# A gate projection by seven block products on one Trainium2 core: sums of h^T ahead of it, and weights split half a task sooner

## The chip, the cores and the metric

The kernel runs on one core of a Trainium2 chip. The metric is the time of one execution on the device, in microseconds (us), lower being better. The engines of the core are TensorE (PE in the profile; PEld is its weight load), VectorE (DVE), ScalarE (ACT), GpSimd (POOL) and SyncE (SP, which here only issues transfers). Each engine works through a queue of its own in a fixed order and waits on semaphores of the others.

## The reference

One layer for 1024 tokens of width 1024, in float32:

```
h = RMSNorm(x)
[q,k,v,z_a | u,z_s | g_a,g_s] = h @ W_in
y_a = BandAttn(q,k,v) * silu(z_a) @ W_attn_out
y_s = GLU(gelu(S5(u))) * silu(z_s) @ W_ssm_out
x = x + (sigmoid(g_a) * y_a + sigmoid(g_s) * y_s) @ W_out
out = RMSNorm(x)
```

The attention and y_a, y_s before their output products are 512 wide; g_a and g_s are 1024 wide. The part that the change rewrites is g_s = h @ W_gs, a product of 1024 by 1024 by 1024.

## The kernel before, in words

**Numbers.** Every large product is made of three matmuls on operands that were split into a rounded high part (hi = round(x), on ACT, line 100) and the rest (lo = x - hi, on DVE, line 103): hi*hi, lo*hi and hi*lo (lines 106 to 108). A weight or an activation is so split once before its use. The normed input is kept transposed as four tiles: hT_134 and hT_135 are the high parts for the halves 0 and 1 of the 1024 features (K), hT_136 and hT_137 the low parts. In a tile lie four K blocks r of 128 features, each with 1024 tokens.

**Tasks.** A projection task makes 128 output columns for all tokens: 8 K blocks x 2 token halves x 3 = 48 matmuls of 512 columns. Its weights come as one load of 512 KB (w_raw), are split into w_hi and w_lo (128x1024 each), and its two halves are evacuated from PSUM by ACT. After the band attention come three tasks for g_a (ga[5:8]), then eight for g_s (`gs_task`, line 1127), whose evacuation is a sigmoid on ACT and a store to DRAM (sgs_dr). Then come tasks with K = 512, of 2 x 4 x 3 = 24 matmuls and one 256 KB load each: 8 for y_a @ W_attn_out ("a tasks": `mm<-y_hi,o_hi` and so on; evacuated on DVE as mgd = mm * sigmoid(g_a)), 8 for the GLU, 8 for y_s @ W_ssm_out, which read the stored sigmoid(g_s) back. Last is the product with W_out, done by pairs of row tiles in seven block products of 12 matmuls (Strassen's scheme in Winograd's form); for it 28 tables `wb` of sums of W_out are made by POOL (sums t, wo_raw), ACT and DVE (splits) while the K = 512 tasks run.

**Stream.** `Stream.run` (line 160 on) keeps the weights of the next task ahead: it loads the raw weights at the start of a task and splits them in its first half (the second task of the 48-matmul kind, after 7 of 16 steps; a K = 512 task has two steps, and the split is put after the first). The splits have high priority.

**Order.** The tile framework sets the order of each engine's queue, from priorities and an estimate of its own; around the attention the kernel places the work by hand. What follows the attention (`issue_after(last_turn)`) is in the part that the framework orders.

Of the kernel before, what the change touches and what calls it, by code (L numbers as in the profile page):

```python
# [17 lines left out]
P = 128  # L18
L = 1024
# [25 lines left out]
def trunk_kernel(ctx: ExitStack, tc: tile.TileContext, x, x_t, ng, w_m, w_v, bias, a_re, a_im, log_dt,  # L45
# [38 lines left out]
    def tt(o, a, b, op, eng=None):  # L84
        (eng or vec).tensor_tensor(out=o, in0=a, in1=b, op=op)  # L85
# [13 lines left out]
    def split_hi(hi, src):  # L99
        act.activation(out=hi, in_=src, func=AF.Copy)  # L100

    def split_lo(lo, src, hi, eng=None):
        (eng or vec).tensor_tensor(out=lo, in0=src, in1=hi.bitcast(F32), op=SUB)  # L103
# [46 lines left out]
    class Stream:  # L150
# [952 lines left out]
    def o_task(src, y, evac, before=None, late=False):  # L1103
# [19 lines left out]
                evac(half, pss[half])  # L1123
                yield
        return (o_dma(src), o_split, run, 2)

    def gs_task(m):
        def evac(half, ps):
            sg = half_tile()
            act.activation(out=sg, in_=ps, func=AF.Sigmoid, bias=gb[:, KT + m:KT + m + 1])  # L1130
# [170 lines left out]
    MATES = {"P1": ("A11", "B11"), "P2": ("A12", "B21"), "P3": ("S4", "B22"), "P4": ("A22", "T4"),  # L1301
             "P5": ("S1", "T1"), "P6": ("S2", "T2"), "P7": ("S3", "T3")}
# [6 lines left out]
    def operand(src, pool_, tag):  # L1309
        t = pool_.tile([P, 2, 4, P], F32R, tag=tag, name="a")  # L1310
        split_hi(t[:, 0], src)
        split_lo(t[:, 1], src, t[:, 0])
        return t
# [12 lines left out]
    ORDER = [("P1", "a", (0,)), ("P2", "b", (0,)), ("P6", "a", (1,)), ("P5", "c", (3,)), ("P7", "a", (3,)),
             ("P3", "c", (1,)), ("P4", "a", (2,))]
# [7 lines left out]
    banks = [(ps_m, "mm")] * 3 + [(ps_2, "s")] * 2 + [(ps_t, "pt")] * 2  # L1341
    taken = [0]

    def bank():
        p_, tag = banks[taken[0] % 7]
        taken[0] += 1
        return p_.tile([P, HALF], F32, tag=tag, name="c")

    for n in range(KT // 2):
        first, last = n == 0, n == KT // 2 - 1  # L1350
        tok = [slice((2 * n + r) * P, (2 * n + r + 1) * P) for r in range(2)]
# [48 lines left out]
        for pn, bk, to in order:  # L1400
            an, bn = MATES[pn]
            if first and an in fin_op:
                a = fin_op[an]
            else:
                for d in DER.get(an, []):
                    derive(*d)
                a = operand(blk[an], vp, "v")
            new = bk not in pss
            if new:
                pss[bk] = bank()  # L1410
            ends = [b for b in to if parts[b] == 1]
            two = last and pn == "P4"
            cuts = [slice(0, HALF)] if not two else [slice(0, HALF // 2), slice(HALF // 2, HALF)]
            for cs in cuts:
                for k in range(4):
                    w = wb[bn, k]
                    o, h, l = pss[bk][:, cs], w[:, 0, cs], w[:, 1, cs]
                    pe.matmul(o, a[:, 0, k, :], h, start=new and k == 0, stop=False, skip_group_check=True)  # L1418
                    pe.matmul(o, a[:, 0, k, :], l, start=False, stop=False, skip_group_check=True)  # L1419
                    pe.matmul(o, a[:, 1, k, :], h, start=False, stop=k == 3, skip_group_check=True)  # L1420
# [84 lines left out]
```

## Time and profile before

| what | value |
|---|---|
| time, median of 3 runs | 810.49 us (809.4 to 811.29) |
| the profiled execution | 809.81 us, with a span of 808.0 us in its trace (1.8 us lie around the span) |
| PE | busy 787.5 us, 97% of the span, 3882 matmuls |
| DVE | busy 515.1 us, 64% |
| ACT | busy 371.4 us, 46% |
| POOL | busy 199.8 us, 25% |
| DMA | 94 GB/s on average |

A row of the timeline gives the start in us, the duration, the engine, the line, the operation, `out<-in` with buffer numbers left out, the size, and in brackets how long the engine had been idle before it and who released it. A matmul's end is modelled: matmuls overlap in the pipeline, so the distance between two starts, and not the duration, says what one costs. A row of the view by windows gives for each engine the busy time in the window and the number of instructions, then the granted PE clock, the share of DMA time and GB/s.

### The profile page before, as it was taken

The numbers are of one execution on the slowest core, as the hardware profiler recorded it, in microseconds if no ns is written. First come the engines' busy times: TensorE is split into PE (matmuls) and PEld (weight loads), VectorE is DVE, ScalarE is ACT, GpSimd is POOL, SyncE is SP. The second block draws the span as 40 slices with busy tenths as digits, with TensorE's granted clock in tenths as the row PEclk, the third lists the DMA queues.
The fourth block names the chain that finished last, engine by engine and source line by source line (L and its number), as shares of the span: only waits on it lengthen the run. The fifth ranks groups of instructions, "written<-read, shape, count | busy, mean of one in ns | idle before, by whom it ended". The sixth has DMA issues, their size and how long they took to land. (4 is left out here: it accounts for less than half of the span.)

```text
span 808.0 us, 11034 instructions
## 1 busy us (share of the span) xinstructions
PE 787.5 (97%) x3882; PEld 652.8 (81%) x3882; DVE 515.1 (64%) x1323; ACT 371.4 (46%) x669; POOL 199.8 (25%) x220
## 2 busy tenths in 40 slices
PE   8999999999999999999999999999999999999996
PEld 6778888888887888888888888888867887788884
DVE  6999997978647888788445430111178337865684
ACT  5653455646436566666444572222253224222542
POOL 4560022020202323333122100000023222844431
PEclk9999999999999999999999999999999999999999
DMA  8703433233331011111000261221144114432232
GB/s 310 263 28 105 116 86 119 90 84 129 102 117 43 27 43 43 44 43 43 27 27 27 79 209 66 104 105 66 52 131 157 52 44 140 132 103 104 104 131 79
DMA packets 37063, 76.22 MB, mean 94 GB/s; under 512 B 5072, under 2 KB 14288, under 8 KB 37008
## 3 DMA queue, kind: packets, MB, share of 16 engines
q1 hardware_dynamic: 32512, 69.74, 25.5%
q0 software_dynamic: 1152, 2.36, 1.4%
q10 hardware_dynamic: 3344, 3.42, 1.4%
q8 instruction: 30, 0.49, 0.3%
q14 instruction: 25, 0.20, 0.1%
HBM read 60.34 MB, written 15.17 MB: 93 GB/s over the span
## 5 line engine op out<-in xcount | busy, mean ns | idle before, releaser
L106 PE MATMUL mm<-hT,w_hi 128*128 128x512 f32 x576 | 233.3, 405 | 0.0
L108 PE MATMUL mm<-hT,w_lo 128*128 128x512 f32 x576 | 226.0, 392 | 0.7 <-DVE w_lo L103 0.7
L107 PE MATMUL mm<-hT,w_hi 128*128 128x512 f32 x576 | 225.4, 391 | 0.0
L108 PEld LDWEIGHTS mm<-hT,w_lo 128*128 128x128 f32 x576 | 108.1, 188 | 24.5 <-DVE w_lo L103 1.1
L107 PEld LDWEIGHTS mm<-hT,w_hi 128*128 128x128 f32 x576 | 108.6, 189 | 16.6 <-issue 0.4
L106 PEld LDWEIGHTS mm<-hT,w_hi 128*128 128x128 f32 x576 | 108.4, 188 | 16.2 <-issue 0.2
L103 DVE TENSOR_TENSOR w_lo<-w_raw,w_hi 128x1024 fp32r<-128x1024 f32 x36 | 44.3, 1230 | 83.7 <-ACT w_hi L100 83.5
L933 POOL TENSOR_SCALAR p<-p,sm 128x640 f32<-128x640 f32 (+2 forms) x64 | 42.8, 671 | 111.2 <-DVE sm L932 80.6
L100 ACT ACTIVATE w_hi<-w_raw 128x1024 fp32r<-128x1024 f32 x36 | 38.1, 1059 | 69.0 <-PE mm L107 58.4
L931 ACT ACTIVATE p<-p,mx 128x640 f32<-128x640 f32 (+2 forms) x64 | 44.5, 695 | 33.3 <-DVE mx L89 16.6
L103 DVE TENSOR_TENSOR tl<-pt,th 128x512 fp32r<-128x512 f32 (+2 forms) x72 | 43.1, 600 | 24.5 <-ACT th L100 23.9
L100 ACT ACTIVATE th<-pt 128x512 fp32r<-128x512 f32 (+2 forms) x72 | 37.7, 523 | 44.5 <-PE pt L951 43.9
L924 DVE CUSTOM_DVE_ANT_0 p<-s,bias 128x320 f32<-128x320 f32 (+2 forms) x96 | 44.2, 485 | 17.1 <-PE s L923 16.7
L106 PE MATMUL mm<-y_hi,o_hi 128*128 128x512 f32 x128 | 50.6, 398 | 3.1 <-DVE sg L85 1.5
L108 PE MATMUL mm<-y_hi,o_lo 128*128 128x512 f32 x128 | 50.5, 396 | 2.6 <-DVE o_lo L103 2.6
L107 PE MATMUL mm<-y_lo,o_hi 128*128 128x512 f32 x128 | 50.4, 394 | 0.0
L85 POOL TENSOR_TENSOR t<-wo_raw 128x512 f32<-128x512 f32 x8 | 11.3, 1409 | 148.7 <-PE mm L107 129.8
L1419 PE MATMUL c<-wb,a 128*128 128x512 f32 (+1 forms) x116 | 44.8, 387 | 0.0
L1418 PE MATMUL c<-wb,a 128*128 128x512 f32 (+1 forms) x116 | 44.1, 386 | 0.5 <-DVE x L85 0.5
L1420 PE MATMUL c<-wb,a 128*128 128x512 f32 (+1 forms) x116 | 44.2, 385 | 0.0
L951 PE MATMUL pt<-ident,p 128*128 128x128 f32 x240 | 38.1, 273 | 0.0
L970 PE MATMUL pv<-tl,vt 128*128 128x256 f32 x144 | 36.2, 281 | 1.0 <-DVE tl L103 1.0
(230 smaller groups left out, 1534.9 us busy)
## 6 DMA issues: line engine op xcount, KB each, us to landing
w_raw<-in_w_m_dram SPq DMA_DIRECT2D x36, 512.0 KB, 3.5
x<-in_x_dram SPq DMA_DIRECT2D x16, 512.0 KB, 7.6
sgs_dr<-sg SPq DMA_DIRECT2D x16, 256.0 KB, 2.0
wo_raw<-in_w_out_dram SPq DMA_DIRECT2D x8, 512.0 KB, 3.5
sg<-sgs_dr SPq DMA_DIRECT2D x16, 256.0 KB, 2.9
xt<-in_x_t_dram SPq DMA_DIRECT2D x6, 512.0 KB, 9.8
bias<-in_bias_dram SPq DMA_DIRECT2D x8, 320.0 KB, 2.9
wv_raw<-in_w_v_dram SPq DMA_DIRECT2D x8, 256.0 KB, 5.4
```

What stands on the lines that cost most here:

```text
L100: act.activation(out=hi, in_=src, func=AF.Copy)
L103: (eng or vec).tensor_tensor(out=lo, in0=src, in1=hi.bitcast(F32), op=SUB)
L106: pe.matmul(ps, lh, rh, start=first, stop=False)
L107: pe.matmul(ps, lh, rl, start=False, stop=False)
L108: pe.matmul(ps, ll, rh, start=False, stop=last)
L924: vec.tensor_tensor_reduce(out=pr[:, c * cw:(c + 1) * cw], in0=ps, in1=bt[:, 640 - w + c * cw:640 - w + (c + 1) * cw], scale=1.0, scalar=- ...
L931: act.activation(out=pr[:, :w], in_=pr[:, :w], func=AF.Exp, bias=mx[:, 0:1], accum_out=sm)
L933: pool.tensor_scalar(out=pr[:, :w], in0=pr[:, :w], scalar1=sm, scalar2=1.0, op0=MUL, op1=MUL)
L951: last_turn[0] = pe.transpose(tp[:, n:n + P], probs[h, q][:, k * P:(k + 1) * P], ident).ins
L1418: pe.matmul(o, a[:, 0, k, :], h, start=new and k == 0, stop=False, skip_group_check=True)
L1419: pe.matmul(o, a[:, 0, k, :], l, start=False, stop=False, skip_group_check=True)
L1420: pe.matmul(o, a[:, 1, k, :], h, start=False, stop=k == 3, skip_group_check=True)
```

## The change

1. The eight `gs_task` are gone. `gs_pairs` does g_s by pairs of column tiles: 4 pairs x 7 block products x 12 matmuls. The left operands are blocks of W_gs and sums of them (S1 to S4 of each pair, four POOL operations a pair), split as 512-wide operands `a`. The right operands are blocks of h^T (B11, B21, B22) and four sums of blocks: T1 = B12 - B11, T3 = B22 - B12, T2 = B22 - T1 and T4 = B21 - T2, each with hi and lo for four K blocks r.
2. `h_sums` makes T1, T2 and T3, a step every second step of the three g_a tasks; T1 and T2 lie in the room of the attention's v (pool vp, tag "v"), two of the T3 tiles in a small pool `gsp`. `h_last` makes T4 in the first four block products, over the second token half of hT_134 and hT_136, which no later product reads. The order of products is P1, P2, P6, P5, P7, P3, P4, where P5 is S1 by T1 and P6 is S2 by T2; the framework may put neighbours the other way round.
3. The evacuation of a block product is an ACT copy into an `sg` tile, a DVE addition (`sg<-c,sg`) or the final sigmoid on ACT.
4. `Stream`: where a K = 512 task follows a K = 512 task, the next weights are split ahead of the first half of the current task (`early`), not after it.
5. Around it: the splits of the attention's output (za, four of 128x1024 hi and lo) go from ahead of the g_a tasks to the 27th block product; the loads `yr` of the S5's output and the first a tasks' weights move with it; the steps at which its splits (`g_lo`) and the W_out tables are emitted shift by some places; the last `zs` tile is split in two halves.

```diff
+        def split(self, task):
+            with tc.high_priority():
+                self.w = task[1](self.raws.pop(id(task)))
...
+                early = ny == 2 and ahead and ahead[0][3] == 2
+                if early:
+                    self.split(ahead[0])
                 for i, _ in enumerate(run(w)):
-                    if i == max(ny // 2 - 1, 0) and ahead:
-                        with tc.high_priority():
-                            self.w = ahead[0][1](self.raws.pop(id(ahead[0])))
+                    if i == max(ny // 2 - 1, 0) and ahead and not early:
+                        self.split(ahead[0])
                     yield
...
-    def gs_task(m):
-        def evac(half, ps):
-            sg = half_tile()
-            act.activation(out=sg, in_=ps, func=AF.Sigmoid, bias=gb[:, KT + m:KT + m + 1])
-            nc.sync.dma_start(out=sgs_dr[m][:, cut(half)], in_=sg)
-        return proj_task(w_m[28 + m], evac)
...
+    def block_product(o, a, tab, cs, first):
+        for k in range(4):
+            h, l = tab(k)
+            pe.matmul(o, a[:, 0, k, :], h[:, cs], start=first and k == 0, stop=False, skip_group_check=True)
+            pe.matmul(o, a[:, 0, k, :], l[:, cs], start=False, stop=False, skip_group_check=True)
+            pe.matmul(o, a[:, 1, k, :], h[:, cs], start=False, stop=k == 3, skip_group_check=True)
...
+    def h_sum(tag, q, r, c, eng):
+
+        o = rest.tile([P, HALF], F32, tag=tag, name="hs")
+        tt(o, hT[0][q][:, r, cut(c)].bitcast(F32), hT[1][q][:, r, cut(c)].bitcast(F32), ADD, eng)
+        return o
+
+    def split_tab(tab, src):
+        split_hi(tab[0], src)
+        split_lo(tab[1], src, tab[0])
+
+    def h_sums():
+
+        for r in range(4):
+            b11 = h_sum("o_raw", 0, r, 0, vec)
+            b12 = h_sum("o_lo", 0, r, 1, vec)
+            b22 = h_sum("o_hi", 1, r, 1, pool)
+            yield
+            tt(b22, b22, b12, SUB, pool)
+            tt(b12, b12, b11, SUB)
+            yield
+            split_tab(h_tab("T3", r), b22)
+            tt(b11, b22, b11, ADD, pool)
+            yield
+            split_tab(h_tab("T1", r), b12)
+            yield
+            split_tab(h_tab("T2", r), b11)
+            yield
+
+    def h_last(r):
+
+        b21 = h_sum("o_raw", 1, r, 0, vec)
+        t2 = rest.tile([P, HALF], F32, tag="o_lo", name="hs")
+        th_, tl_ = h_tab("T2", r)
+        tt(t2, th_.bitcast(F32), tl_.bitcast(F32), ADD, pool)
+        tt(b21, b21, t2, SUB, vec)
+        split_tab(h_tab("T4", r), b21)
...
+        with tc.high_priority():
+            g_op[u] = operand(src.rearrange("p (k m) -> p k m", m=P), wp, tag)
+        if pn == "P2":
+
+            g_s1[n] = rest.tile([P, HALF], F32, tag="o_hi", name="s1")
+            a11, a12, a21, a22 = (g_block(b, n) for b in ("A11", "A12", "A21", "A22"))
+            tt(g_s1[n], a21, a22, ADD, pool)
+            tt(a21, a11, a21, SUB, pool)
+            tt(a11, g_s1[n], a11, SUB, pool)
+            tt(a12, a12, a11, SUB, pool)
+
+    def gs_pairs():
+
+        AHEAD = 2
+        for u in range(AHEAD):
+            g_operand(u)
+        yield
...
+            if u + AHEAD < steps:
+                g_operand(u + AHEAD)
+            if n == 0 and i < 4:
+                h_last(i)
+            new = (n, bk) not in pss
+            if new:
+                pss[n, bk] = bank()
+            ps = pss[n, bk]
+            block_product(ps, g_op.pop(u), lambda k: h_tab(MATES[pn][1], k), slice(0, HALF), new)
...
+    gen = stream.run(ga[NGA:])
+    sums = h_sums()
+    n_ga = len(ga[NGA:]) * 2 * KT
+    for n in range(n_ga):
+        with tc.issue_after(last_turn[0]) if n < 4 * KT else ExitStack():
             next(gen)
-    for b in range(2):
-        load_y(b)
+        if n % 2 == 1:
+            next(sums, None)
...
-    hs, ls = split_tiles(zs, vp, "v", "y")
+    hs, ls = split_tiles(zs, vp, "v", "y", (3,))
```

The order of three queues at the place where g_s begins. First DVE, from the last operation of the attention (`y<-pv,y`) on; `hs` are sums of blocks of h^T, `t_...` their splits into the tables. Before:

```order
985 L103 TENSOR_TENSOR w_lo<-w_raw,w_hi 128x1024
986 L85 TENSOR_TENSOR y<-pv,y 64x512
987 L103 TENSOR_TENSOR y_lo<-z,y_hi 128x1024
988 L103 TENSOR_TENSOR o_lo<-o_raw,o_hi 128x512 x2
989 L103 TENSOR_TENSOR w_lo<-w_raw,w_hi 128x1024 x9
```

In the changed kernel:

```order
981 L103 TENSOR_TENSOR w_lo<-w_raw,w_hi 128x1024
982 L85 TENSOR_TENSOR y<-pv,y 64x512
983 L85 TENSOR_TENSOR hs<-hT_134,hT_136 128x512 x4
984 L85 TENSOR_TENSOR hs<-hs 128x512
985 L103 TENSOR_TENSOR t_5183<-hs,t_5183 128x512
986 L85 TENSOR_TENSOR hs<-hs 128x512
```

And the end of what stands there ahead of the operands of the first pair's third and fourth product (`a<-g_raw,a` in row 1017 is S2 for P6, `a<-s_5430,a` in row 1018 is S1 for P5):

```order
1011 L85 TENSOR_TENSOR hs<-hT_135,hT_137 128x512
1012 L103 TENSOR_TENSOR hT_136<-hs,hT_134 128x512
1013 L85 TENSOR_TENSOR hs<-hs 128x512
1014 L85 TENSOR_TENSOR hs<-hT_135,hT_137 128x512
1015 L85 TENSOR_TENSOR hs<-hs 128x512
1016 L103 TENSOR_TENSOR hT_136<-hs,hT_134 128x512
1017 L103 TENSOR_TENSOR a<-g_raw,a 128x512
1018 L103 TENSOR_TENSOR a<-s_5430,a 128x512
```

Between the last `y` and the operand of P5 stood nothing; now stand 39 operations there (one of them the third g_a task's w_lo of 128x1024; rows with x4 or x2 are so many), and the operand is the 40th. The first operand of g_s (P1) is the 23rd.

POOL, from the last operation of the attention (`z<-z,y`) on. Before:

```order
107 L933 TENSOR_SCALAR p<-p,sm 128x640 x3
108 L85 TENSOR_TENSOR z<-z,y 64x512 x2
109 L85 TENSOR_TENSOR t<-wo_raw 128x512
110 L85 TENSOR_TENSOR wo_raw<-wo_raw 128x512
111 L85 TENSOR_TENSOR t<-wo_raw 128x512
```

Changed (`s_5430` is S1; the `g_raw<-s_5430,g_raw` of row 119 makes S2):

```order
108 L85 TENSOR_TENSOR z<-z,y 64x512 x2
109 L85 TENSOR_TENSOR hs<-hT_135,hT_137 128x512 x2
110 L85 TENSOR_TENSOR hs<-hs 128x512 x4
111 L85 TENSOR_TENSOR hs<-hT_135,hT_137 128x512 x2
112 L85 TENSOR_TENSOR hs<-hs 128x512 x3
113 L85 TENSOR_TENSOR hs<-t_5175 128x512
114 L85 TENSOR_TENSOR s_5430<-g_raw 128x512
115 L85 TENSOR_TENSOR hs<-hs 128x512
116 L85 TENSOR_TENSOR g_raw<-g_raw 128x512
117 L85 TENSOR_TENSOR hs<-t_5176 128x512
118 L85 TENSOR_TENSOR hs<-t_5177 128x512
119 L85 TENSOR_TENSOR g_raw<-s_5430,g_raw 128x512
```

Where POOL went from the attention straight to the tables of W_out, it now has 18 operations up to S2, all of 128x512 with both inputs in SBUF.

PE, 24 matmuls after the last g_a matmul. Before, in the first task of g_s:

```order
2217 L106 MATMUL mm<-hT_135,w_hi 128x512
2218 L107 MATMUL mm<-hT_137,w_hi 128x512
2219 L108 MATMUL mm<-hT_135,w_lo 128x512
2220 L106 MATMUL mm<-hT_134,w_hi 128x512
2221 L107 MATMUL mm<-hT_136,w_hi 128x512
```

Changed, where P2 ends and P5 begins, whose right operand is T1 (t_5179 and the three after it):

```order
2217 L1225 MATMUL c<-hT_135,a 128x512
2218 L1226 MATMUL c<-hT_137,a 128x512
2219 L1227 MATMUL c<-hT_135,a 128x512
2220 L1225 MATMUL c<-t_5179,a 128x512
2221 L1226 MATMUL c<-t_5179,a 128x512
```

P1 and P2 take h^T as it is; P5 stands third, with P6 after it, so that S1's operand is the first for which PE needs the end of the DVE rows above.

More of the change, by code (lines that the diff above doesn't have):

```diff
@@ L1070, in trunk_kernel, with split_tiles @@
     sgs_dr = [dr.tile([P, L], F32, name=f"sgs_dr{m}") for m in range(KT)]
+    gsp_cm = tc.tile_pool(name="gsp", reuse_waits="tile", bufs=2)
+    gsp = gsp_cm.__enter__()
+    half_pool = [gsp, 3]
     def half_tile():
-        return rest.tile([P, HALF], F32, tag="sg", name="sg", bufs=4)
+        return half_pool[0].tile([P, HALF], F32, tag="sg", name="sg", bufs=half_pool[1])
     def cut(half):
         return slice(half * HALF, (half + 1) * HALF)
-    def split_tiles(raws, pool_, tag, name):
+    def split_tiles(raws, pool_, tag, name, halves=()):
         hs, ls = [], []
-        for r in raws:
+        for n, r in enumerate(raws):
             hi = pool_.tile([P, L], F32R, tag=tag, name=name + "_hi")
             lo = pool_.tile([P, L], F32R, tag=tag, name=name + "_lo")
-            split_hi(hi, r)
-            split_lo(lo, r, hi)
+            for c in [cut(0), cut(1)] if n in halves else [slice(0, L)]:
+                split_hi(hi[:, c], r[:, c])
+                split_lo(lo[:, c], r[:, c], hi[:, c])
             hs.append(hi)
@@ new lines, in trunk_kernel, with bank, operand @@
+    taken = [0]
+    def bank():
+        p_, tag = banks[taken[0] % 7]
+        taken[0] += 1
+        return p_.tile([P, HALF], F32, tag=tag, name="c")
+    def operand(src, pool_, tag):
+        t = pool_.tile([P, 2, 4, P], F32R, tag=tag, name="a")
+        split_hi(t[:, 0], src)
+        split_lo(t[:, 1], src, t[:, 0])
+        return t
+    def block_product(o, a, tab, cs, first):
[4 more added lines that the diff above has]
+            pe.matmul(o, a[:, 1, k, :], h[:, cs], start=False, stop=k == 3, skip_group_check=True)
@@ new lines, in trunk_kernel, with h_tab @@
+    t2s = [vp.tile([P, 2, HALF], F32R, tag="v", name="t2") for _ in range(4)]
+    t1s = [vp.tile([P, 2, HALF], F32R, tag="v", name="t1") for _ in range(4)]
+    t3s = [qk_pools[1].tile([P, 2, HALF], F32R, tag="blk", name="t3") for _ in range(2)] + [
+        gsp.tile([P, 2, HALF], F32R, tag="t3", name="t3") for _ in range(2)]
+    def h_tab(name, r):
+        if name in ("B11", "B21", "B22", "T4"):
+            q, c = (0 if name in ("B11", "T4") else 1), cut(1 if name in ("B22", "T4") else 0)
+            return hT[0][q][:, r, c], hT[1][q][:, r, c]
+        t = {"T1": t1s, "T2": t2s, "T3": t3s}[name][r]
+        return t[:, 0, :], t[:, 1, :]
@@ new lines, in h_last, with g_load @@
+    def h_last(r):
[5 more added lines that the diff above has]
+        split_tab(h_tab("T4", r), b21)
+    g_raw = {}
+    def g_load(m):
+        p_, tag, b = (wp, "w_raw", 1) if m % 3 == 0 else (rows, "yr", 2)
+        g_raw[m] = p_.tile([P, D], F32, tag=tag, name="g_raw", bufs=b)
+        with tc.high_priority():
+            nc.sync.dma_start(out=g_raw[m], in_=w_m[28 + m])
@@ new lines, in g_block, with g_operand @@
+    def g_block(name, n):
+        m = 2 * n + int(name[1]) - 1
+        return g_raw[m][:, cut(int(name[2]) - 1)]
+    g_op = {}
+    g_s1 = {}
+    turn_op = [0]
+    def g_operand(u):
+        n, pn = u // 7, ORDER[u % 7][0]
+        place = {"P1": "A11", "P2": "A12", "P6": "A11", "P7": "A21", "P3": "A12", "P4": "A22"}
+        src = g_s1[n] if pn == "P5" else g_block(place[pn], n)
+        tag = ("w_hi", "w_lo")[turn_op[0] % 2]
+        turn_op[0] += 1
+        with tc.high_priority():
+            g_op[u] = operand(src.rearrange("p (k m) -> p k m", m=P), wp, tag)
[6 more added lines that the diff above has]
+            tt(a12, a12, a11, SUB, pool)
@@ new lines, in gs_pairs, with done @@
+    def gs_pairs():
[3 more added lines that the diff above has]
+        yield
+        pss, out_ = {}, {}
+        steps = 7 * KT // 2
+        for u in range(steps):
+            n, i = u // 7, u % 7
+            pn, bk, to = ORDER[i]
+            if n < KT // 2 - 1 and i in (1, 4):
+                m = 2 * n + (2 if i == 1 else 3)
+                if m not in g_raw:
+                    g_load(m)
+            if u + AHEAD < steps:
[7 more added lines that the diff above has]
+            block_product(ps, g_op.pop(u), lambda k: h_tab(MATES[pn][1], k), slice(0, HALF), new)
+            def done(b, o):
+                m, half = 2 * n + b // 2, b % 2
+                act.activation(out=o, in_=ps if b == 2 else o, func=AF.Sigmoid, bias=gb[:, KT + m:KT + m + 1])
+                nc.sync.dma_start(out=sgs_dr[m][:, cut(half)], in_=o)
+            if pn in ("P1", "P6", "P5"):
+                b = to[0]
+                out_[b] = half_tile()
+                act.activation(out=out_[b], in_=ps, func=AF.Copy)
+            elif pn == "P4":
+                done(2, half_tile())
+            else:
+                b = to[0]
+                o = out_.pop(b)
+                tt(o, ps, o, ADD)
+                done(b, o)
+            yield
@@ L1201, in load_y @@
         ygr.append(yr)
-    gen = stream.run(ga[NGA:] + [gs_task(m) for m in range(KT)], a_all[:2])
-    for _ in range(4 * KT):
-        with tc.issue_after(last_turn[0]):
-            next(gen)
-    for b in range(2):
-        load_y(b)
+    gen = stream.run(ga[NGA:])
[3 more added lines that the diff above has]
+        with tc.issue_after(last_turn[0]) if n < 4 * KT else ExitStack():
+            next(gen)
+        if n % 2 == 1:
+            next(sums, None)
+        if n == n_ga - 12:
+            g_load(1)
+            g_load(2)
+        if n == n_ga - 9:
+            g_load(0)
     for _ in gen:
         pass
+    for u, _ in enumerate(gs_pairs()):
+        if u == 20:
+            load_y(0)
+        if u == 25:
+            for t in a_all[:2]:
+                stream.load(t)
+        if u == 26:
+            load_y(1)
+            hs, ls = split_tiles(za, vp, "v", "y")
+            ya[0].extend(hs)
+            ya[1].extend(ls)
+    stream.split(a_all[0])
+    gsp_cm.__exit__(None, None, None)
+    late_cm = tc.tile_pool(name="late", reuse_waits="tile", bufs=2)
+    late = late_cm.__enter__()
+    half_pool[:] = [late, 4]
     wp_cm.__exit__(None, None, None)
@@ L1250, in sum_tile @@
         def sum_tile():
-            return rest.tile([P, HALF], F32, tag="t", name="t", bufs=1)
+            return late.tile([P, HALF], F32, tag="t", name="t", bufs=1)
         b11, b12 = raws[j][0][:, cut(0)], raws[j][0][:, cut(1)]
@@ L1287, in trunk_kernel @@
     for n, _ in enumerate(stream.run(a_all, glu[:2])):
-        if n < 4:
-            split_y_ssm(n)
+        if n in (0, 1, 5, 6):
+            split_y_ssm(len(yg[0]))
             if n < 2:
                 load_y(n + 2)
-        elif n > 4:
+        elif n > 6:
             next(tables)
     for n, _ in enumerate(stream.run(glu, so_all[:2])):
-        if n >= 2 and len(wb) < 16:
+        if n >= 3 and len(wb) < 16:
             next(tables)
-    hs, ls = split_tiles(zs, vp, "v", "y")
+    hs, ls = split_tiles(zs, vp, "v", "y", (3,))
     ys[0].extend(hs)
@@ L1307, in block @@
         return mgd[int(name[2]) - 1][:, :, t * P:(t + 1) * P]
[L1309 to L1313, printed above, removed]
     for n, _ in enumerate(stream.run(so_all)):
@@ L1319, in trunk_kernel @@
             fin_op["A11"] = operand(block(0, "A11"), rows, "yr")
-            s3 = rest.tile([P, HALF], F32, tag="t", name="s3", bufs=1).rearrange("p (k m) -> p k m", m=P)
+            s3 = late.tile([P, HALF], F32, tag="t", name="s3", bufs=1).rearrange("p (k m) -> p k m", m=P)
             tt(s3, block(0, "A11"), block(0, "A21"), SUB, pool)
@@ L1323, in trunk_kernel @@
     assert len(wb) == 28
+    late_cm.__exit__(None, None, None)
     rest_cm.__exit__(None, None, None)
[L1332 to L1333 removed]
     FIRST = [("P1", "a", (0,)), ("P7", "d", (3,)), ("P2", "b", (0,)), ("P6", "a", (1, 2, 3)), ("P5", "c", (3,)),
@@ L1340, in trunk_kernel @@
     nc.scalar.dma_start(out=fg_b, in_=fg.partition_broadcast(P))
[L1341 to L1347, printed above, removed]
     for n in range(KT // 2):
@@ L1414, in trunk_kernel @@
             for cs in cuts:
[L1415 to L1420, printed above, removed]
+                block_product(pss[bk][:, cs], a, lambda k: (wb[bn, k][:, 0, :], wb[bn, k][:, 1, :]), cs, new)
                 for b in to:
```

10 lines of the change are left out of this document (5 added, 5 removed).

## The prediction, on record before the change was run

> **What bounds the kernel now.** I read the page's busy line first, then the view by windows around g_s, then single rows of the timeline.
>
> ```profile
> PE 787.5 (97%) x3882; PEld 652.8 (81%) x3882; DVE 515.1 (64%) x1323; ACT 371.4 (46%) x669; POOL 199.8 (25%) x220
> ...
> 474.00:494.00 20.00, 20.00 (x90) 16.57 (x89) 4.65 (x5) 8.76 (x14) 0.00 (x0) 1.00 0.30 105
> 494.00:514.00 20.00, 20.00 (x90) 16.57 (x89) 2.45 (x2) 4.89 (x7) 0.00 (x0) 1.00 0.27 93
> 514.00:580.00 66.00, 66.00 (x293) 54.64 (x292) 6.13 (x5) 13.01 (x17) 0.00 (x0) 1.00 0.22 80
> ```
>
> PE is the bound, and in the g_a and g_s tasks (474 to 580) it is the only one: 20.00 of 20 us busy, while DVE works 2.45 of 20 us and POOL not at all. So each matmul taken out there is worth its full time, and DVE and POOL have room. What a matmul costs is the distance of starts, not the 0.39 us of its record:
>
> ```profile
> 493.63 0.39 PE L106 MATMUL mm<-hT,w_hi 128*128 128x512 f32 x1
> ...
> 580.67 0.39 PE L106 MATMUL mm<-y_hi,o_hi 128*128 128x512 f32 x1
> ```
>
> The first is the first matmul of g_s, the second the first one after g_s: 87.04 us for 384 matmuls, 0.2267 us each, without a gap.
>
> **The matmuls removed.** g_s has 336 in place of 384. 48 x 0.2267 = **-10.9 us**. (By the duration of the record it would be 48 x 0.39 = 18.7, but the records overlap.)
>
> **What must be ready, and when.** The cost is in the sums of h^T. They start when the attention lets go of DVE and POOL:
>
> ```profile
> 465.54 0.69 DVE L85 TENSOR_TENSOR y<-pv,y 64x512 f32<-64x512 f32 x1
> ...
> 466.31 1.30 POOL L85 TENSOR_TENSOR z<-z,y 64x512 f32<-64x512 f32 x1 [16.57 <-DVE y L85]
> 597.36 1.44 POOL L85 TENSOR_TENSOR t<-wo_raw 128x512 f32<-128x512 f32 x1 [129.75 <-PE mm L107]
> ```
>
> DVE is free at 466.2, POOL at 467.6, and POOL then has no work for 129.75 us. PE reaches the first product at 493.6 and, 24 matmuls or 5.4 us later, P5 at 499.1. By the order of the changed queues, P5's operand is the 40th DVE operation from 466.2 on; ahead of it, or needed by it or its neighbour, POOL has 18. All of these have both inputs in SBUF. So 40 and 18 operations have 33 us. Prices of one alone, and of two together:
>
> ```profile
> 605.12 1.28 DVE L103 TENSOR_TENSOR wb<-wo_raw,wb 128x512 fp32r<-128x512 f32 x2
> 606.33 0.68 DVE L103 TENSOR_TENSOR o_lo<-o_raw,o_hi 128x512 fp32r<-128x512 f32 x1
> ...
> L103 DVE TENSOR_TENSOR w_lo<-w_raw,w_hi x36: 1205/1224/1471, 56.7 to 560.0; 128x1024 fp32r<-128x1024 f32 x36
> L85 POOL TENSOR_TENSOR z<-z,y x16: 1274/1289/1298, 264.3 to 466.3; 64x512 f32<-64x512 f32 x16
> ...
> L85 POOL TENSOR_TENSOR mgd<-mgd,sg x14: 1288/1700/1755, 686.2 to 717.2; 128x512 f32<-128x512 f32 x14
> L103 DVE TENSOR_TENSOR wb<-wo_raw,wb x20: 674/1200/1782, 597.9 to 698.2; 128x512 fp32r<-128x512 f32 x20
> L85 DVE TENSOR_TENSOR sg<-mm,sg x16: 673/680/692, 683.7 to 722.6; 128x512 f32<-128x512 f32 x16
> ```
>
> The grouped rows give least/median/most in ns. Alone, a DVE operation of this size takes a place of (606.33 - 605.12)/2 = 0.605 us, w_lo 1.22, a POOL operation 1.29. Where POOL works too, POOL's median is 1.70, and DVE's `wb` goes up to 1.78. DVE's `sg<-mm,sg`, which reads PSUM, stays at 0.68 in the same stretch. The rows of that stretch show what happens:
>
> ```profile
> 694.32 1.74 POOL L85 TENSOR_TENSOR wo_raw<-wo_raw,t 128x512 f32<-128x512 f32 x1
> 696.02 3.44 POOL L85 TENSOR_TENSOR mgd<-mgd,sg 128x512 f32<-128x512 f32 x2
> ...
> 693.13 1.78 DVE L103 TENSOR_TENSOR wb<-wo_raw,wb 128x512 fp32r<-128x512 f32 x1
> 694.83 0.68 DVE L85 TENSOR_TENSOR sg<-mm,sg 128x512 f32<-128x512 f32 x1
> 695.43 1.18 DVE L103 TENSOR_TENSOR wb<-wo_raw,wb 128x512 fp32r<-128x512 f32 x1
> 696.53 0.68 DVE L85 TENSOR_TENSOR sg<-mm,sg 128x512 f32<-128x512 f32 x1
> 697.13 1.18 DVE L103 TENSOR_TENSOR o_lo<-o_raw,o_hi 128x512 fp32r<-128x512 f32 x1
> ```
>
> POOL's starts are 694.32, 696.02 and 697.74: one per 1.70 us. In each such period DVE gets one operation with two SBUF inputs done, and it ends 0.55 us behind POOL's end (694.32 + 1.74 = 696.06, `wb` ends at 696.61). So they take turns: 1.15 for POOL, 0.55 for DVE, and neither hides under the other.
>
> **The sum for the sums.** If they are parallel, DVE needs 39 x 0.605 + 1.22 = 24.8 us, to 491.0, and POOL 18 x 1.29 = 23.2, to 490.8: both in time. If they take turns, 18 turns x 1.70 = 30.6, the 21 other DVE operations 12.7 and w_lo 1.22: 44.5 us, to 510.7. To this come the hand-overs, since the chain of each K block r goes from POOL to DVE to ACT to DVE and back. One costs:
>
> ```profile
> 597.89 1.46 DVE L103 TENSOR_TENSOR wb<-wo_raw,wb 128x512 fp32r<-128x512 f32 x1 [0.24 <-ACT wb L100]
> ```
>
> Eight rounds (four in h_sums, four in h_last) with one open hand-over or a little more, some ten at 0.24, make 2.4 us: 513.1. PE then waits 513.1 - 499.1 = **+14.0 us**, nearly all ahead of P5 (the first product's own operand is the 23rd on DVE with 10 on POOL: 10 x 1.70 + 12 x 0.605 + 1.22 = 25.5, at 491.7, with a few hand-overs just before or behind 493.6). Below, the wait is bounded by the parallel case: T4's splits stand ahead of P5's operand on DVE and write where the last g_a matmul (493.6) still reads; from there an ACT split and nine DVE places, 0.63 + 9 x 0.605 = 6.1, to 499.7, leave about 1 us. Above, with every POOL operation at its 1.74 and every DVE operation at 0.605 behind it, 18 x 2.35 + 12.7 + 1.2 + 2.4 = 58.6, to 524.8, they leave 26. I take 14, since the 1.70 is the row of two full queues, which is what stands here.
>
> The Trainium skill has a rule for this ("SBUF — State Buffer", section "SBUF: two separate sides"): a DVE operation with two SBUF inputs and a GpSimd operation that reads SBUF lock a shared port pair for the whole instruction, and the other one is blocked fully. By it a turn is 1.29 + 0.605 = 1.90, and 18 turns are 3.5 us more than by the rows, so that the wait would be 17.5. The rows agree that one excludes the other, but show 1.70 a turn, and I go by them.
>
> **The clock after the wait.** A shorter idle stretch in the a tasks shows what follows:
>
> ```profile
> 607.00:610.40 3.40, 3.34 (x9) 2.70 (x10) 2.41 (x5) 0.49 (x1) 0.36 (x1) 0.57 0.80 245
> ...
> 607.65 0.63 PE L106 MATMUL mm<-y_hi,o_hi 128*128 128x512 f32 x1
> 608.08 0.63 PE L107 MATMUL mm<-y_lo,o_hi 128*128 128x512 f32 x1
> ```
>
> The granted clock is 0.57 in this window, and matmuls start 0.43 apart, not 0.2267, for about 3 us: some 7 matmuls x 0.20 = 1.4 us lost. After 14 us of waiting the same is due once: **+1.5**, between 0 and 3 (two such stretches).
>
> **The rest of g_s.** A pair takes 84 x 0.2267 = 19.0 us on PE. In that time DVE has seven splits, of which four beside POOL's four sums, and three additions from PSUM: 4 x 1.70 + 3 x 0.605 + 3 x 0.68 = 10.7. ACT has seven splits at 0.63 and seven copies and sigmoids at 0.69:
>
> ```profile
> L100 ACT ACTIVATE w_hi<-w_raw x36: 1046/1061/1064, 52.8 to 558.9; 128x1024 fp32r<-128x1024 f32 x36
> L100 ACT ACTIVATE wb<-t x8: 614/632/636, 598.8 to 691.4; 128x512 fp32r<-128x512 f32 x8
> L1130 ACT ACTIVATE sg<-mm,gb x16: 668/688/692, 499.3 to 580.9; 128x512 f32<-128x512 f32 x16
> ...
> w_raw<-in_w_m_dram SPq DMA_DIRECT2D x36, 512.0 KB, 3.5
> ```
>
> That is 9.2 us. Both fit under PE's 19.0 in the pairs two to four; if they did not, each would cost its excess, and there is none to 8 us. The loads are the same eight of 512 KB, asked for most of a pair ahead, against the 3.5 us of the last row. The za splits that move to the 27th product (four of 1.06 and 1.22) fit there too. **0**.
>
> **Weights half a task sooner.** The waits of PE in the a tasks, and from there to 720, are:
>
> ```profile
> PE mm L108 <- DVE o_lo L103: 1.4, 1, 1.4
> PE mm L106 <- ACT o_hi L100: 1.1, 1, 1.1
> PE mm L106 <- DVE mgd L85: 0.5, 1, 0.5
> ...
> PE mm L106 <- DVE sg L85: 1.5, 1, 1.5
> PE mm L108 <- DVE o_lo L103: 1.2, 1, 1.2
> ...
> 600.00:612.00 12.00, 9.00 (x32) 6.48 (x31) 9.49 (x13) 5.13 (x9) 5.16 (x4) 0.86 0.38 128
> ```
>
> In the a tasks there are 3.0 us and the 1.4 of the clock behind them. At best all 4.4 goes. But in 600 to 612 DVE works 9.49 and POOL 5.16 of 12 us: by the turns above they are full, and an o_lo that goes sooner makes the evacuation `mgd` behind it later, for which the next half waits. At worst each of seven a tasks waits the 1.1 of the row: +7.7 - 4.4 = +3.3. I take **+1**, since the work is the same and W_out's tables begin two steps later and so closer together. For the later pair of waits (2.7), the last zs tile in halves brings its first half about 0.6 + 0.6 us forward (half of 1.06 and of 1.22): **-1**, between -2.7 and 0.
>
> **Sum.** -10.9 + 14.0 + 1.5 + 0 + 1 - 1 = +4.6. The profiled execution's 809.8 (span 808.0 and 1.8 around it) becomes 814.4. It lies 0.7 below the median of the runs shown, so on that footing **815 us**, 0.6% slower.
>
> **Rivals.** (1) The sums hide under the g_a tasks: DVE and POOL run side by side and PE waits about 1 us. For it: 466 to 494 is empty on both, by the windows. Against it: the row of 1.70 us. 809.8 - 10.9 + 1 + 0 + 0.7 = **800.6**, down to 797 if the 4.4 of the a tasks goes too. This is the other side. (2) They exclude each other, but less: DVE's operations fit in while POOL waits for its inputs, and half the 44.5 - 24.8 = 19.7 us is saved; the wait is 14 - 10 = 4 to 8 us. 809.8 - 10.9 + 6 + 1.5 + 0.7 = **807**, to 810. (3) The turns take the full time of both, as in the upper bound, on half of the turns (9 x 0.65 = +5.8), or each a task waits (+2.3 more than I took): 815 + 6 = **821**. (4) The early split does not do what it says, since the framework orders the splits anyway: then the a tasks lose or gain nothing, which is within the main case.
>
> **Chances.** Main case 0.60, with a range of its own from 811 to 821; rival 1 0.18; rival 2 0.12; rival 3 0.10. The range to hold 8 in 10 goes from 800 (half of rival 1 and all of rival 2) to 822. About 0.2% (1.6 us) is what a measurement here can tell from no change. Faster is rival 1 and two thirds of rival 2: 0.25. Same is the rest of rival 2 and 0.04 of the main case: 0.08. Slower 0.67.
>
> **What would show it.** Right: in the changed profile a wait of PE of 10 to 17 us for DVE's `a<-s_...` (or an ACT split of it) about 5 us into g_s, a clock of about half just after it, and in the stretch before it POOL `hs` of 1.3 to 1.75 and DVE `hs` stretched above 1.1 us. After that 84 matmuls per 19.0 us. Wrong: DVE `hs` at 0.68 beside a busy POOL, P5 starting by 501, and a span 8 to 12 us below 808.0; or waits of over 1 us in the second pair; or PE waits in the a tasks that sum to over 7 us or to nothing.

## The result

The changed kernel takes 821.49 us (median of 4 runs, 820.58 to 823.70); the kernel before, on the same chip, 810.34 us (median of 4). The ratio is 1.0143, with a 95% interval of 1.0126 to 1.0160: 11.2 us slower, where the prediction had 4.6. Two of all the executions on record, one of the kernel before and one of e7 below, took 974 and 1074 us at a mean granted clock of 0.75 and 0.67; they are left out of every time and ratio here. The profiled execution of the changed kernel has a span of 820.4 us, 12.4 more than that of the kernel before. The first line of its page, busy time, share and number of instructions of each engine:

```profile
PE 782.8 (95%) x3834; PEld 644.4 (79%) x3834; DVE 576.3 (70%) x1392; ACT 394.7 (48%) x718; POOL 249.4 (30%) x252
```

PE has 48 matmuls less and 4.7 us less of busy time, but a span that is longer: 2 points of its share have become waits. The view of what PE waited for, from 470 to 730 us (total, times, longest), of the changed kernel:

```profile
PE c L1225 <- ACT mg L998: 11.7, 1, 11.7
PE mm L106 <- DVE mgd L85: 3.7, 4, 2.1
PE mm L108 <- DVE o_lo L103: 3.6, 4, 1.5
PE c L1227 <- DVE a L103: 2.1, 1, 2.1
PE mm L106 <- ACT sg L1342: 0.8, 1, 0.8
PE mm L106 <- DVE sg L85: 0.2, 1, 0.2
```

The first and the fourth row are new and belong to the first pair of g_s (13.8 us). The others are in the K = 512 tasks: 8.3 us, where the kernel before had 5.7. PE's timeline of the changed kernel at the two new waits:

```profile
496.52 0.50 PE L1227 MATMUL c<-hT,a 128*128 128x512 f32 x1 [2.06 <-DVE a L103]
496.86 0.40 PE L1225 MATMUL c<-hT,a 128*128 128x512 f32 x1
...
501.58 0.39 PE L1227 MATMUL c<-hT,a 128*128 128x512 f32 x1
513.68 0.80 PE L1225 MATMUL c<-t,a 128*128 128x512 f32 x1 [11.71 <-ACT mg L998]
514.27 0.63 PE L1226 MATMUL c<-t,a 128*128 128x512 f32 x1
514.70 0.64 PE L1227 MATMUL c<-t,a 128*128 128x512 f32 x1
```

P1's operand is 2.06 us late and P5 starts 11.7 us late, at 513.7. After it matmuls start 0.43 apart: the clock is at half. The release of P5 is put down to an evacuation of the last g_a task (`mg`) on ACT, but that is only the end of a queue: in the timeline of ACT, a split of T4 stands ahead of it that had itself waited 3.91 us for a sum on DVE, and S1's split (`a<-s`), which P5 needs as well and which ends at 513.05, stands between them:

```profile
511.38 0.63 ACT L100 ACTIVATE hT<-hs 128x512 fp32r<-128x512 f32 x1 [3.91 <-DVE hs L85]
511.92 0.61 ACT L100 ACTIVATE a<-g_raw 128x512 fp32r<-128x512 f32 x1
512.44 0.61 ACT L100 ACTIVATE a<-s 128x512 fp32r<-128x512 f32 x1
512.96 0.67 ACT L998 ACTIVATE mg<-mm,gb 128x512 f32<-128x512 f32 x1
```

What held DVE is in the grouped view of the sums (`hs`) and their splits (`t`), least/median/most in ns, of the changed kernel, DVE first and then POOL:

```profile
L85 DVE TENSOR_TENSOR hs<-hT,hT x12: 679/1164/1787, 466.5 to 511.2; 128x512 f32<-128x512 f32 x12
L103 DVE TENSOR_TENSOR t<-hs,t x12: 677/1774/1784, 475.2 to 502.7; 128x512 fp32r<-128x512 f32 x12
L85 DVE TENSOR_TENSOR hs<-hs x8: 676/1140/1781, 473.5 to 512.0; 128x512 f32<-128x512 f32 x8
...
L85 POOL TENSOR_TENSOR hs<-hs x8: 1283/1737/2209, 471.7 to 495.9; 128x512 f32<-128x512 f32 x8
L85 POOL TENSOR_TENSOR hs<-t x4: 1581/1658/1670, 492.6 to 506.9; 128x512 f32<-128x512 f32 x4
```

These are the stretched times of the two engines side by side: a 0.68 us operation takes a median of 1.14 to 1.77 on DVE, a 1.29 us operation 1.66 to 1.74 on POOL.

By stages, from the starts of PE's matmuls in the two profiled executions:

| stretch | before, us | changed, us | difference |
|---|---|---|---|
| up to the first matmul of g_s | 493.6 | 493.9 | +0.2 |
| g_s and the 24 matmuls of the first a task | 92.5 | 98.3 | +5.8 |
| the other seven a tasks | 43.7 | 47.7 | +4.0 |
| GLU | 44.8 | 44.8 | 0 |
| from there to the last matmul | 125.6 | 128.0 | +2.4 |

(The changed kernel runs the first a task's matmuls among the last pair of g_s, so the two are taken together.) The +5.8 are the 48 matmuls (-10.9), the waits (+14.1 of start-to-start distance over the normal one), the half clock behind P5 (+1.6) and 1.0 that is left, most of it a slightly longer distance of the block products' matmuls (0.8 in e6, below). The +2.4 at the end holds a stretch at half clock of 1.6 us that an execution of the same instruction queues (e1, below) does not have: there the last stretch is 125.7.

### The profile page after: what moved, and what is told of

It reads as the page before. It is cut to its first block, busy times and chain, and to the rows that moved or that the text cites. A ratio compares the mean times of both kernels' runs of the same rounds, so it can differ in the third digit from the quotient of the medians.

```text
span 820.4 us, 11150 instructions
## 1 busy us (share of the span) xinstructions
PE 782.8 (95%) x3834; PEld 644.4 (79%) x3834; DVE 576.3 (70%) x1392; ACT 394.7 (48%) x718; POOL 249.4 (30%) x252
## 5 line engine op out<-in xcount | busy, mean ns | idle before, releaser
L106 PE MATMUL mm<-hT,w_hi 128*128 128x512 f32 x448 | 183.5, 410 | 0.0
L108 PE MATMUL mm<-hT,w_lo 128*128 128x512 f32 x448 | 176.3, 394 | 0.6 <-DVE w_lo L103 0.6
L107 PE MATMUL mm<-hT,w_hi 128*128 128x512 f32 x448 | 175.6, 392 | 0.0
L108 PEld LDWEIGHTS mm<-hT,w_lo 128*128 128x128 f32 x448 | 84.1, 188 | 19.6 <-DVE w_lo L103 1.1
L107 PEld LDWEIGHTS mm<-hT,w_hi 128*128 128x128 f32 x448 | 84.6, 189 | 11.6 <-issue 0.4
L106 PEld LDWEIGHTS mm<-hT,w_hi 128*128 128x128 f32 x448 | 84.4, 188 | 11.2 <-issue 0.2
L100 ACT ACTIVATE w_hi<-w_raw 128x1024 fp32r<-128x1024 f32 x28 | 29.6, 1058 | 38.9 <-PE mm L107 28.3
L1225 PE MATMUL c<-wb,a 128*128 128x512 f32 (+1 forms) x116 | 44.5, 387 | 0.8 <-DVE x L85 0.8
L103 DVE TENSOR_TENSOR w_lo<-w_raw,w_hi 128x1024 fp32r<-128x1024 f32 x28 | 34.5, 1231 | 15.0 <-ACT w_hi L100 14.8
L1226 PE MATMUL c<-wb,a 128*128 128x512 f32 (+1 forms) x116 | 44.8, 387 | 0.0
L975 PE MATMUL pv<-th,vt 128*128 128x256 f32 x144 | 36.1, 272 | 0.2
```

The source lines that it names most:

```text
L106: pe.matmul(ps, lh, rh, start=first, stop=False)
L107: pe.matmul(ps, lh, rl, start=False, stop=False)
L108: pe.matmul(ps, ll, rh, start=False, stop=last)
L1225: pe.matmul(o, a[:, 0, k, :], h[:, cs], start=first and k == 0, stop=False, skip_group_check=True)
L1226: pe.matmul(o, a[:, 0, k, :], l[:, cs], start=False, stop=False, skip_group_check=True)
```

## The experiments

Two questions: is the wait in the first pair due to DVE and POOL excluding each other, and what costs the a tasks their 4 us? All ratios are to the kernel before on the same chip.

**e1, the early split undone.**

```diff
-                early = ny == 2 and ahead and ahead[0][3] == 2
+                early = False
```

> The changed kernel with the early split of the K = 512 weights undone (they are split after the first half of a task again). The queues of all five engines read the same with and without it, since the splits have high priority and the framework puts them where it put them before. Theory A (the early split does nothing): 821.5 within 1.5 us, the waits of PE in the a tasks as in the changed kernel (about 8 us). Rival (the early split is what costs the a tasks their 4 us, by putting o_lo ahead of the evacuations): 816 to 818.

Measured: 822.13 us, ratio 1.0133 (1.0117 to 1.0149), the same as the changed kernel. PE's longer waits in the a tasks are the same ones (1.0, 0.8, 1.1, 2.2 and 0.7 us of excess distance in the places where the changed kernel has 0.6, 0.8, 1.1, 2.3 and 0.7). So the early split does nothing: all five queues read the same without it. The loss in the a tasks is not its work.

**e3, POOL's sums of h^T on DVE** (four places like this one):

```diff
-            b22 = h_sum("o_hi", 1, r, 1, pool)
+            b22 = h_sum("o_hi", 1, r, 1, vec)
-            tt(b22, b22, b12, SUB, pool)
+            tt(b22, b22, b12, SUB)
```

> The changed kernel with the 16 sums of h^T that POOL made put on DVE; POOL keeps only the sums of the weights. Theory (DVE and POOL take turns, 1.70 us a pair): P5's operand is the 45th operation on DVE, 45 x 0.605 + 0.6 + 3 turns x 1.1 = 31 us after 466.2, at 497.5; PE's wait of 14 us falls to 0 to 4, the half clock behind it goes, 821.5 - 10 - 1.5 = 806 to 811. Rival (the time lies in hand-overs between engines or in work, not in turns; DVE gets 16 operations more): the wait stays at 12 or grows, 820 to 830.

Measured: 807.82 us, ratio 0.9963 (0.9950 to 0.9976). DVE has 16 operations more and the kernel is 13.7 us faster than the changed one. The waits for P1 and P5 are gone; what is left in g_s is one of 2.04 us, with a half clock behind it, at the fifth product in PE's order:

```profile
509.15 0.50 PE L1227 MATMUL c<-hT,a 128*128 128x512 f32 x1 [2.04 <-DVE a L103]
```

Its right operand lies in the tiles of h^T, so it isn't P6, whose right operand T2 has tiles of its own (`t`); the expectations of e6 and e7 below call it P6's. The split that it waits for stands on DVE behind the turns with POOL's four sums of W_gs. The grouped view of DVE in this kernel:

```profile
L85 DVE TENSOR_TENSOR hs<-hT,hT x16: 676/680/1793, 468.0 to 507.2; 128x512 f32<-128x512 f32 x16
L85 DVE TENSOR_TENSOR hs<-hs x16: 676/680/682, 472.8 to 509.0; 128x512 f32<-128x512 f32 x16
L103 DVE TENSOR_TENSOR t<-hs,t x12: 676/678/1787, 476.3 to 495.4; 128x512 fp32r<-128x512 f32 x12
```

The medians, 1.14 to 1.77 in the changed kernel, are 0.68 here. The same work on one engine takes less time than on two.

**e4, POOL writes the same tiles but reads nothing.** Its 16 sums are fills with zeros under the same waits; the sums, and with them sigmoid(g_s), are left out of the computation.

```diff
-            tt(b22, b22, b12, SUB, pool)
+            pool.memset(b22, 0.0)
-            tt(b11, b22, b11, ADD, pool)
+            pool.memset(b11, 0.0)
```

> The changed kernel with each of the 16 sums of h^T on POOL put in place by a POOL fill with zeros of the same tile: POOL writes as many tiles under the same waits, but reads none (the sums and with them sigmoid(g_s) are left out of the computation). Theory (the two engines exclude each other when both read SBUF): DVE's hs and t go at 0.60 to 0.68 each, POOL's fill is not stretched, the wait ahead of P5 is 0 to 2 us, 805 to 810. Rival (any POOL operation, or the hand-overs, hold DVE up): the wait stays above 8 us, DVE's operations above 1.1 us where POOL works, 816 or more.

Measured: 806.28 us, ratio 0.9938 (0.9918 to 0.9957). The wait ahead of P5 is 0.28 us. The grouped view, DVE and then POOL:

```profile
L85 DVE TENSOR_TENSOR hs<-hT,hT x12: 680/689/1793, 468.0 to 498.8; 128x512 f32<-128x512 f32 x12
L103 DVE TENSOR_TENSOR t<-hs,t x12: 685/690/1796, 474.4 to 493.0; 128x512 fp32r<-128x512 f32 x12
...
L1263 POOL MEMSET hs<- x4: 526/526/527, 470.8 to 476.9; 128x512 f32 x4
```

The fills run beside DVE's operations in 0.53 us each, all alike, and DVE's median is 0.69; the few long DVE operations stand beside POOL's sums of W_gs and its last `z<-z,y`, which still read. So it is not POOL's being busy, its writing or the hand-overs that hold up DVE's operations with two SBUF inputs; what the sums do and the fills don't is read. (A fill is also shorter than a sum, so the gain to 806 is not all the exclusion; the durations are what decides.) The Trainium skill ("SBUF — State Buffer", section "Who interferes with whom") says that a DVE instruction with two SBUF inputs contends with a GpSimd instruction that reads SBUF and not with one that only writes it; this run agrees, with 0.53 and 0.69 us.

**e5, another room for T3.** The first evacuation of the a tasks in the changed kernel has a wait that the kernel before has not. DVE's timeline in the changed kernel:

```profile
590.05 0.69 DVE L103 TENSOR_TENSOR o_lo<-o_raw,o_hi 128x512 fp32r<-128x512 f32 x1 [0.66 <-ACT o_hi L100]
595.26 1.89 DVE L85 TENSOR_TENSOR mgd<-mm,mg 128x512 f32<-128x512 f32 x3 [4.52 <-DMA sgs_dr<-sg]
597.07 3.95 DVE L103 TENSOR_TENSOR g_lo<-yr,g_hi 128x1024 fp32r<-128x1024 f32 x2
```

DVE stands idle for 4.52 us because `mgd` waits for a store of sigmoid(g_s) to land. In the experiment the two T3 tiles lie above the sg tiles in memory, in a pool of their own, so that the room that is reused next is T3's:

```diff
+    gst_cm = tc.tile_pool(name="gst", reuse_waits="tile", bufs=2)
+    gst = gst_cm.__enter__()
     half_pool = [gsp, 3]
...
-        gsp.tile([P, 2, HALF], F32R, tag="t3", name="t3") for _ in range(2)]
+        gst.tile([P, 2, HALF], F32R, tag="t3", name="t3") for _ in range(2)]
```

> The changed kernel with the two T3 tiles in a pool of their own above the sg tiles, so that the room of the accumulator mgd no longer lies over the last sg tiles. In the changed kernel the first evacuation of the a tasks stands on DVE until the last store of sigmoid(g_s) has landed (4.5 us idle, to 595.3). Theory A (this wait makes the S5 splits and with them the tables of W_out late and crowds them, which is most of the 4 us lost in the a tasks): first mgd at about 593, the first table operation on POOL 2 us sooner, 818 to 820. Rival (the loss is the turns of POOL's tables and DVE whatever their start): 821.5 within 1 us.

Measured: 819.11 us, ratio 1.0096 (1.0077 to 1.0115), 2.4 us less than the changed kernel, whose interval (1.0126 to 1.0160) lies above this one, and 3.0 less than e1, which has the changed kernel's queues and ran on the same chip as e5. DVE's timeline in e5:

```profile
591.20 0.69 DVE L103 TENSOR_TENSOR o_lo<-o_raw,o_hi 128x512 fp32r<-128x512 f32 x1 [0.66 <-ACT o_hi L100]
591.81 1.28 DVE L85 TENSOR_TENSOR mgd<-mm,mg 128x512 f32<-128x512 f32 x2
596.18 3.99 DVE L103 TENSOR_TENSOR g_lo<-yr,g_hi 128x1024 fp32r<-128x1024 f32 x2 [3.09 <-ACT g_hi L100]
```

`mgd` follows without a wait, and the seven a tasks take 44.5 us, against 47.7 in the changed kernel and 43.7 before: 3.2 of the 4.0 us. The room of the freed pool was the larger part of that loss. Part of the 3.2 is a stretch at half clock in the changed kernel (matmuls 0.43 apart from 634.0 to 636.1, some 1.5 us), which e5 does not have and e1 has; its longest wait in these tasks is 1.1 us, not 2.1. The first table operation on POOL starts 1.2 us sooner (611.19 to 610.01) where 2 were expected, though PE begins these tasks 1.1 us later in e5. About as much as the 0.8 that is left is a wait of 0.83 us for an evacuation of g_s on ACT (`sg`, L1342 in the changed kernel), at the first matmul of these seven tasks; the kernel before does not have it, e5 and e6 do.

**e6, all of POOL's work after the attention on DVE**, with the room of e5: the sums of h^T (as e3), of W_gs and of W_out, and

```diff
-        tt(merged(m, cut(half)), merged(m, cut(half)), sgs[half], ADD, pool if m < KT - 1 else vec)
+        tt(merged(m, cut(half)), merged(m, cut(half)), sgs[half], ADD, vec)
-        tt(zs[m][:, sl], zs[m][:, sl], sgs[half], MUL, pool if m < 3 else vec)
+        tt(zs[m][:, sl], zs[m][:, sl], sgs[half], MUL, vec)
```

> The changed kernel with everything that POOL does after the attention put on DVE (the sums of h^T, of W_gs and of W_out, the products with z_s and the additions to mgd), and the T3 tiles in a pool of their own. Theory (turns): the waits ahead of the first pair are gone, the a tasks and the last K = 512 tasks lose less: 807.8 - 2.4 (the room) - 3.8 (P6's wait and the half clock behind it) - 2 to 4 = 798 to 801. Rival (DVE becomes the bound where it has over 20 of 24 us of work): 805 or more, with waits of PE for DVE of over 8 us after g_s.

Measured: 797.28 us, ratio 0.9845 (0.9830 to 0.9859): faster than both kernels, by 12.7 and 24.2 us, and 0.7 below the range that was expected. What PE still waits for from 470 to 730:

```profile
PE mm L108 <- DVE o_lo L103: 1.7, 2, 1.1
PE mm L106 <- ACT sg L1344: 0.8, 1, 0.8
PE mm L106 <- ACT wb L100: 0.5, 1, 0.5
```

3.0 us in place of 22.1, and no stretch at half clock. In the window of g_s (493.4 to 575.7) PE is busy throughout, in that of the a tasks 39.2 of 41.7 us, while POOL does nothing, and DVE, with POOL's operations added, still has room:

```profile
493.40:575.70 82.30, 82.30 (x361) 67.35 (x359) 50.29 (x76) 41.35 (x66) 0.00 (x0) 1.00 0.39 131
575.70:617.40 41.70, 39.20 (x169) 31.41 (x169) 33.95 (x47) 20.60 (x26) 0.00 (x0) 1.00 0.46 150
```

**e7, the sums of h^T and of W_gs on DVE, with the room of e5**; the tables of W_out, zs and mgd stay on POOL. Its edits are those of e3 and e5 and the four sums of a pair.

> The changed kernel with the sums of h^T and of W_gs on DVE and the T3 tiles in a pool of their own; the rest of POOL's work stays. Theory: g_s runs without a wait of over 1 us, and the first evacuation of the a tasks doesn't wait for a store: 807.8 - 2.4 - 3.8 = 801 to 803. Rival (the clock's dip and P6's wait come from DVE's added work): 805 or more.

Measured: 803.42 us (802.22 to 804.42, 3 runs), ratio 0.9917 (0.9898 to 0.9936). No profile of it is read, so that only its time speaks. It lies 0.4 above the 801 to 803 of the theory and below the rival's 805, some 4 us below e3. What separates it from e6 are the edits in the K = 512 tasks alone: some 6 us.

**e8, the kernel before with its POOL work after the attention on DVE** (the edits of e6 for W_out, zs and mgd; g_s by tasks as before).

> The kernel before with POOL's work after the attention put on DVE (sums of W_out, products with z_s, additions to mgd), g_s as it was. Theory (turns cost the K = 512 tasks of the kernel before too): its waits of 8.7 us in these tasks, the half clock included, fall to 4 to 6: 806 to 808. Rival (there the turns are hidden): 810 within 1 us, or slower, since DVE has more to do.

Measured: 805.60 us, ratio 0.9942 (0.9928 to 0.9957). That is a little below the 806 to 808 expected. PE's waits from 470 to 730 fall from 5.7 to 1.5 us, and the half clock behind them is gone:

```profile
PE mm L106 <- DVE mgd L85: 1.0, 2, 0.8
PE mm L108 <- DVE o_lo L103: 0.5, 1, 0.5
```

So having that work on POOL cost the kernel before 4.4 us as well (809.97 on the same chip, less 805.60). It is also the fair base for the block products: between e8 and e6 lie 8.3 us (805.60 - 797.28), of the 10.9 that the matmuls are worth.

## Why the prediction was right or wrong

**The matmuls removed: right, a little too much.** 48 x 0.2267 = 10.9. In e6, where g_s has no wait of PE, its 336 matmuls and the 24 of the first a task take 82.15 us for 359 distances, 0.2288 each and not 0.2267. That is 0.8 us for all of them. Why the distance is longer was not looked into.

**The sum for the sums: right in its mechanism, and in its size partly by luck.** The prediction had P5 at 513.1 and 14.0 us of wait; it started at 513.7, and the waits make 14.1. The turns that it counted from the 1.70 us of another stage are there, and e3 and e4 show that they are the cause. But S1's split on DVE, which the prediction put at 513.1, starts at 513.81, and POOL has run 20 operations by then and not 18:

```profile
508.43 1.71 POOL L85 TENSOR_TENSOR g_raw<-g_raw 128x512 f32<-128x512 f32 x1
...
513.81 0.69 DVE L103 TENSOR_TENSOR a<-s,a 128x512 fp32r<-128x512 f32 x1
```

The first row is the 20th; the 19th, at 506.89, is the fourth of the sums `hs<-t`, which T4 needs and the prediction left out. Against that, DVE stood waiting for only 1.2 us, where the prediction gave the hand-overs 2.4. An estimate from these counts, 20 x 1.70 + 19 x 0.605 + 1.22 + 1.2 = 47.9 us, agrees with the 48.0 from DVE's first sum (466.48) to the end of S1's split (514.50). Sum by full blocking, 17.5 us of wait by the rule of the Trainium skill ("SBUF — State Buffer", section "SBUF: two separate sides") that the prediction set beside it, was too long: the turns overlap a little, as the rows of the kernel before had shown. The prediction put a wait for P1 "just before or behind 493.6"; it was 2.06 us of the total.

**The clock after the wait: right.** The windows of the changed kernel around P5:

```profile
499.40:513.60 14.20, 2.57 (x12) 1.74 (x10) 13.82 (x15) 4.00 (x8) 8.27 (x5) 0.75 0.00 0
513.60:517.00 3.40, 3.32 (x8) 2.48 (x9) 3.28 (x6) 3.04 (x7) 0.00 (x0) 0.53 0.56 132
```

A granted clock of 0.53 for 3.4 us, and 1.6 us lost in this execution (1.5 forecast); in the one of e1, with the same queues, 12 matmuls and 2.5 us.

**The rest of g_s: right.** From 517 to 592 PE is busy throughout (75.00 of 75):

```profile
517.00:592.00 75.00, 75.00 (x329) 61.41 (x328) 30.04 (x41) 34.69 (x55) 16.51 (x12) 1.00 0.42 137
```

**Weights half a task sooner: this step failed.** It took +1 for the a tasks and -1 for the last tasks; measured were +4.0 and +2.4 in the profiled execution. These 6.4 us are most of the 7.8 by which that execution lies above the forecast (12.4 against 4.6); another 1.0 is what was left over in g_s. The step failed in three points.

First, its subject: the early split moves nothing (e1). Rival 4 had named that, but gave it no price of its own. The order of the queues would have shown it: behind the first a tasks, DVE runs two evacuations and then one weight split (`o_lo`) in both kernels.

Second, and this is the size: it priced the splits and left out the rooms. The change closes a pool with the sg tiles and opens the accumulator's over it, and so the first evacuation waits for a store (4.52 us of DVE idle). The prediction has no term for it. Behind it the S5 splits, the tables of W_out and the evacuations are all later against PE, which had run the first a task ahead. The waits for mgd rise from 0.5 to 3.7 us. Taking the room away (e5) returns 3.2 of the 4.0 in the profiled executions, some 1.5 of it a half clock that goes with the waits, and 2.4 to 3.0 us of the time.

Third, what the last zs tile in halves brings forward did not shorten the end: PE's wait for `sg` fell from 1.5 to 0.2, but its waits for `o_lo` there are 0.9 and 1.5 where there was one of 1.2. The last stretch is 125.7 in e1, as before the change (125.6); the +2.4 of the changed kernel's own profile is for 1.6 us a half clock after one of these waits.

**The range and the chances.** The main case, the wait of 14 us, is what happened, and the time lies just beyond the upper edge of that case's own range (811 to 821) and inside the whole one (to 822). The size of the slowing was missed by a factor of 2.4: 4.6 against 11.2 us. Rival 1, that the sums hide, holds only if POOL does not read (e4), or does none of the sums (e3).

## What to carry to other kernels

Work for an idle GpSimd is not free work: where DVE has operations with two SBUF inputs at the same time, count a pair of 128x512 float32 operations as 1.70 us against 1.21 for both on DVE, and give GpSimd only what DVE doesn't run beside, or reads nothing. Count the operations that stand in queue ahead of the first operand that the bound engine needs, and the time between, before a gain in matmuls is booked. When a pool is closed and another is opened in its place, look up which tiles lie in the reused room and what reads or stores them last.

## What the runs showed of the hardware that was not expected

**A train of DVE operations kept POOL out until it ended, once.** In the rows from which the prediction took the turns, the two engines alternate. In e4 they did not at one place; POOL's timeline and then DVE's:

```profile
482.92 5.89 POOL L85 TENSOR_TENSOR s<-g_raw 128x512 f32<-128x512 f32 x1 [0.64 <-DVE t L103]
488.88 1.29 POOL L85 TENSOR_TENSOR g_raw<-g_raw 128x512 f32<-128x512 f32 x1
...
483.35 0.69 DVE L85 TENSOR_TENSOR hs<-hT,hT 128x512 f32<-128x512 f32 x1
...
485.76 0.69 DVE L85 TENSOR_TENSOR hs<-hT,hT 128x512 f32<-128x512 f32 x1
486.36 1.29 DVE L103 TENSOR_TENSOR a<-g_raw,a 128x512 fp32r<-128x512 f32 x2
```

POOL's sum started within a train of DVE operations that follow each other every 0.60 us until 487.65, and ended only 1.16 us after that, 5.89 us in all; DVE was not stretched. What decides between this and the turns was not tried.

**The half clock comes after quite different waits.** A wait of 2.06 us (at 496.5 in the changed kernel) was not followed by it, one of 2.04 us in e3 was, and one of 1.48 us was in the changed kernel but not in e1 at the same matmul. The timelines, of the changed kernel:

```profile
710.50 0.50 PE L108 MATMUL mm<-y_hi,o_lo 128*128 128x512 f32 x1 [1.48 <-DVE o_lo L103]
...
711.64 0.63 PE L106 MATMUL mm<-y_hi,o_hi 128*128 128x512 f32 x1
712.07 0.63 PE L107 MATMUL mm<-y_lo,o_hi 128*128 128x512 f32 x1
```

and of e1:

```profile
712.01 0.50 PE L108 MATMUL mm<-y_hi,o_lo 128*128 128x512 f32 x1 [1.48 <-DVE o_lo L103]
712.35 0.40 PE L106 MATMUL mm<-y_hi,o_hi 128*128 128x512 f32 x1
712.59 0.39 PE L107 MATMUL mm<-y_lo,o_hi 128*128 128x512 f32 x1
```

So in these runs a wait of 1.5 to 2.1 us had either no price on top or some 1.6 us, and two executions of the same queues differed by it. What decides was not tried.
